# Third layer of a four-layer network: where the two tail steps of a region stand in the stream of matrix products

## The chip, the cores and the metric

One core of a Trainium2 chip runs the whole program. The metric is device time in microseconds (us), the median of several executions. TensorE (PE) does the matrix products, VectorE (DVE) and ScalarE (ACT) the elementwise work, GpSimd (POOL) a few copies, and SyncE (SP) issues the transfers.

## What is computed

Four layers over 1040 tokens (16 meta tokens and 1024 of the input) of width 1024: sliding-window attention, a matrix LSTM, a gated linear recurrence (HGRN2), and attention again. The change lies in the third. Per head, with chunks of tokens, its recurrence is, cut to what matters:

```python
def step(S, inp):
    q_, k_, v_, lf = inp
    A = jnp.cumsum(lf, axis=2)
    o_inter = jnp.einsum('bhtd,bhde->bhte', q_ * jnp.exp(A), S)
    dec = jnp.where(causal[..., None], A[:, :, :, None, :] - A[:, :, None, :, :], -jnp.inf)
    att = jnp.einsum('bhtd,bhtsd,bhsd->bhts', q_, jnp.exp(dec), k_)
    o = o_inter + jnp.einsum('bhts,bhse->bhte', att, v_)
    A_last = A[:, :, -1]
    S_new = jnp.exp(A_last)[..., None] * S + jnp.einsum('bhsd,bhse->bhde', k_ * jnp.exp(A_last[:, :, None] - A), v_)
    return S_new, o
```

The output of a chunk needs the state S that the chunk before it left. Before the recurrence the inputs are projected, after it the output is normed, gated with silu(z) and projected back.

## The kernel before, in words

Tokens lie in the columns: a block of 16 (block 0) and eight blocks of 128, in three column chunks of 400, 384 and 256. Each projection multiplies three times (high and low halves of the operands, `proj` L237, `proj_v` L271, `proj_out` L308). These products fill TensorE, and the recurrence of the third layer is woven between them.

`layer_c` (L1049) treats eight heads (0 to 7 here). A head has five regions (`REGIONS`, L1126): block 0 alone, then four pairs of blocks. `mixer` (L1128) makes two lists of steps for each region r. The main list holds eight level steps (`level`, L1139: DVE and ACT make the scaled keys and queries X), one burst of small products (`levels_mm`, L1181) and `tail0` (L1185), which masks and sums the products into the matrix `att` (DVE L1195 and L1204, POOL copies L1206, ACT copies L1208 and L1210) and makes the scaled queries `qA` and keys `kA`. The tail list holds `tail1` (L1222: TensorE transposes `kA` into PSUM, L1228, and ACT copies that to `kT`, L1230), a lag of 500, and for each block of the region one `tail2` (L1232). A `tail2` issues three products: `att` with the values (L1243), the scaled queries with the state S (L1245), and keys with values (L1250). From the last one DVE makes the next state (L1253 and L1255). One `kT` tile and two S tiles exist; PSUM has eight tiles for all uses.

Each step is a list of a cost, a function and a load. `weave` (L53) merges two lists so that both advance in proportion to their summed costs. The tail list of region r is woven with the main list of region r+1, behind a lag of 2000 (`TAIL_LAG`); the result is woven with the projections of the next head (the fill). The order of TensorE's instructions is exactly this order. The other engines' orders come from the framework's scheduler, which takes steps marked by `hi` (L356) early. Every engine runs its own instructions in that order and waits where an operand is missing. `pause` (L768) is a function that does nothing; the second layer already uses it as a step that counts in a weave and is taken out behind it.

Of the kernel before, what the change touches and what calls it, by code (L numbers as in the profile page):

```python
# [15 lines left out]
P = 128  # L16
# [5 lines left out]
NB = 9  # L22
# [7 lines left out]
def blk(b):  # L30
    return (0, NMETA) if b == 0 else (NMETA + P * (b - 1), P)
# [5 lines left out]
TAIL_LAG = 2000.0  # L37
# [1 line left out]
ROWS, TMPS, RAWS, YS, QS = 9, 5, 2, 3, 6  # L39
XS = 14  # L40
GAP, BURST, PAUSE = 200.0, 1300.0, 2500.0
KT_LAG = 500.0
NORM_AT = (4000.0, 0.7), (5000.0, 0.5), (8000.0, 0.5)
Y_LAST, Y_EARLY, Y_AHEAD = 3, 8, 2500.0
PARTS = 2, 2, 2
# [7 lines left out]
def weave(a, b):  # L53

    ta, tb = sum(x[0] for x in a) + 1e-9, sum(x[0] for x in b) + 1e-9
    out, i, j, ca, cb = [], 0, 0, 0.0, 0.0
    while i < len(a) or j < len(b):
        if j >= len(b) or (i < len(a) and ca / ta <= cb / tb):
            ca += a[i][0]
            out.append(a[i])  # L60
            i += 1
        else:
            cb += b[j][0]
            out.append(b[j])
            j += 1
    return out


def flat(groups):
    return [x for grp in groups for x in grp]  # L70


def outs(groups):

    first, out = groups[0]
    out = list(out)
    for splits, grp in groups[1:]:
        out.insert(len(out) - Y_EARLY, splits[0])
        out.insert(len(out) - Y_LAST, splits[1])
        out += grp  # L80
    return first, out
# [27 lines left out]
def hybrid_kernel(ctx: ExitStack, tc: tile.TileContext, ins, out, layers=(0, 1, 2, 3)):  # L109
    nc = tc.nc  # L110
    v, s, g, pe, sp = nc.vector, nc.scalar, nc.gpsimd, nc.tensor, nc.sync
# [11 lines left out]
    def nm(x):  # L123
        ctr[0] += 1
        return f"{x}{ctr[0]}"

    def row():
        return rpool.tile([P, T], F32, tag="r", name=nm("r"), bufs=ROWS)
# [13 lines left out]
    def psum(tag, bufs):  # L142
        return ps.tile([P, 512], F32, tag="p", name=nm(tag), bufs=8)
# [4 lines left out]
    def psa():  # L148
        return psum("pa", 1)
# [206 lines left out]
    def hi(fn):  # L356
        def f():
            with tc.high_priority(offset=PRIO):
                fn()

        return f
# [687 lines left out]
    def layer_c(i, j, fin):  # L1049
# [78 lines left out]
        def mixer(h):  # L1128
            vs = slice((h % 2) * P, (h % 2) * P + P)
            W = {}  # L1130
# [101 lines left out]
            def tail2(r, b):  # L1232
                blkno = REGIONS[r][b]
                c0, cn = blk(blkno)
                n = [blkno in z for z in CHUNK_BLOCKS].index(True)
                if blkno == CHUNK_BLOCKS[n][0]:
                    if n == 0:
                        R["o", h] = row()
                    W["po"] = psum("po", 1)
                oc = slice(c0 - CHUNKS[n][0], c0 - CHUNKS[n][0] + cn)  # L1240
                V = R["v", h // 2, blkno]
                att = W["att", r] if r == 0 else W["att", r][:, b, :]
                pe.matmul(W["po"][:, oc], V[:cn, vs], att, start=True, stop=(r == 0))  # L1243
                if r:
                    pe.matmul(W["po"][:, oc], W["S"], W["qA", r][:, P * b : P * b + P], start=False, stop=True)  # L1245
                if blkno == CHUNK_BLOCKS[n][-1]:
                    o_evac(n)
                if blkno < NB - 1:
                    pc = psa()
                    pe.matmul(pc[:, :P], W["kT", r][:cn, P * b : P * b + P], V[:cn, vs], start=True, stop=True)  # L1250
                    Sn = R["mix"].tile([P, P], F32, tag="S", name=nm("S"), bufs=2)
                    if r == 0:
                        v.tensor_copy(Sn, pc[:, :P])  # L1253
                    else:
                        v.scalar_tensor_tensor(Sn, W["S"], W["eL", r][:, b : b + 1], pc[:, :P],  # L1255
                                               op0=ALU.mult, op1=ALU.add)
                    W["S"] = Sn

            def o_evac(n):
                c0, cn = CHUNKS[n]  # L1260
                s.copy(R["o", h][:, c0 : c0 + cn], W["po"][:, :cn])
                W["sq", n] = sq = tmp()
                s.activation(sq[:, :cn], W["po"][:, :cn], AF.Square)
# [9 lines left out]
            def S(cost, fn, *a):  # L1273
                return [cost, hi(lambda: fn(*a)), None]

            main, tails = [], []
            for r in range(5):
                lvs = list(range(8)) if r else [3, 4, 5, 6, 7]
                st = []
                for lv in lvs:  # L1280
                    st.append(S(0.0, level, r, lv))
                    st.append([GAP, lambda: None, None])
                st.append(S(BURST if r else 0.2 * BURST, levels_mm, r, lvs))
                st.append(S(0.0, tail0, r))
                main.append(st)
                ts = [S(214 if r else 107, tail1, r), [KT_LAG, lambda: None, None]]
                for b in range(len(REGIONS[r])):
                    ts.append(S(640, tail2, r, b))
                    if REGIONS[r][b] in (5, 8):
                        ts.append(S(666, o_stat, 0 if REGIONS[r][b] == 5 else 1))  # L1290
                tails.append(ts)
# [10 lines left out]
        body = qg[0][0] + qg[0][1]  # L1302
        last = []
        for h in range(8):
            fill = qg[0][2] if h == 0 else []
            if h in (4, 6):
                fill += flat(outs(oc[h - 3]))
            if h < 7:
                fill += flat(fg[h + 1]) + flat(qg[h + 1])
            if h in (1, 3, 5):  # L1310
                fill += flat(vg[h // 2 + 1])
            for z in {2: (0, 1), 4: (2,), 5: (3,), 7: (4, 5, 6)}.get(h, ()):
                fill += flat(zg[z])
            main, tails, end = mixer(h)
            if h:
                tails[0].append(held)
            held = end
            mx = []
            for r in range(5):
                mx += weave(main[r], last)  # L1320
                last = [[TAIL_LAG, lambda: None, None]] + tails[r]
            body += weave(mx, fill)
        body += weave(last + [held], flat(zg[7]))
        return head, body, oc[5], oc[7]

    steps = []
# [4 lines left out]
    for pos, i in enumerate(layers):  # L1331
# [10 lines left out]
        if i % 3 == 0:  # L1342
            head, body, oa, ob = layer_a(i, i // 3, tail is None, i == 3, fin)
        elif i % 3 == 1:
            head, body, oa, ob = layer_b(i, i // 3, fin)
        else:
            head, body, oa, ob = layer_c(i, i // 3, fin)
# [158 lines left out]
```

## Time and profile before

| | us |
|---|---|
| median of 3 runs | 2607.71 (2605.75 to 2611.24) |
| the profiled execution | 2610.83 |
| its span, first to last instruction | 2609.0 |
| PE busy in the span | 2558.0 (98%) |
| DVE busy | 1980.3 (76%) |
| ACT busy | 1725.9 (66%) |
| POOL busy | 154.1 (6%) |

The span is the time from the first to the last instruction of the profiled execution; 1.8 us of that execution lie outside it. PE is the matrix products, PEld the loading of their stationary operand, which runs beside them. The third layer's recurrence takes the stretch from about 1611 to 2120 us of the span, some 62 us per head.

### The profile page before, as it was taken

What the parts mean: (1) busy time and instruction counts of PE and PEld (TensorE: products, weight loads), DVE (VectorE), ACT (ScalarE), POOL (GpSimd) and SP (SyncE); (2) the same over time, 40 slices, a digit from 0 to 9 for tenths busy, and PEclk for the clock granted to TensorE, in tenths of its full rate; (3) what the DMA queues carried; (4) which work ended last, traced back from release to release, by engine and by line L of the source; (5) the groups of instructions that cost most, each with busy time, mean ns of one, the idle gap of its engine ahead of it and who ended that gap; (6) DMA issues with size and microseconds to landing.
All of it is one profiled execution on the core that took longest, in us unless ns stands there. A gap on an engine that the chain in (4) does not pass through costs nothing.

```text
span 2609.0 us, 56062 instructions
## 1 busy us (share of the span) xinstructions
PE 2558.0 (98%) x21048; PEld 2459.0 (94%) x21048; DVE 1980.3 (76%) x5487; ACT 1725.9 (66%) x4757; POOL 154.1 (6%) x538
## 2 busy tenths in 40 slices
PE   7999999999999999999999999999999999999999
PEld 6899889899999999999999999999999999999999
DVE  6677777986767676767677788978787978677776
ACT  6777776566464646464646857878585867768872
POOL 1100100000000000000000000201001011000000
PEclk9999999999999999999999999999999999999999
DMA  4111111021111111111110101011110111111112
GB/s 136 56 43 50 46 37 47 17 67 58 41 58 41 58 41 58 41 58 41 55 61 34 57 27 42 30 38 34 34 42 26 42 62 45 54 44 47 53 38 82
DMA packets 74048, 126.81 MB, mean 49 GB/s; under 512 B 11552, under 2 KB 25760, under 8 KB 73776
## 3 DMA queue, kind: packets, MB, share of 16 engines
q1 hardware_dynamic: 73776, 123.23, 14.5%
q8 instruction: 165, 2.70, 0.4%
q14 instruction: 107, 0.88, 0.1%
HBM read 108.34 MB, written 4.26 MB: 43 GB/s over the span
## 4 chain that ended last, share of the span: by engine, by line
PE 81%; DVE 10%; ACT 6%; issue 1%; DMA 1%; POOL 0%; SPq 0%; DVEq 0%; ACTq 0%; POOLq 0%
PE pj L254 39%; PE pj L337 16%; PE pj L299 11%; PE po L682 2%; PE pt L660 1%; PE pm L614 1%; PE pm L615 1%; DVE t L407 1%; PE pa L534 1%; DVE ul L188 1%; PE po L918 1%; PE pj L295 1%; PE pm L890 1%; DVE X L1153 1%; DVE X L1155 1%
## 5 line engine op out<-in xcount | busy, mean ns | idle before, releaser
L254 PE MATMUL pj<-uh,wh 128*128 128x384 f32 (+2 forms) x2592 | 870.9, 336 | 3.7 <-ACT uh L187 3.6
L254 PE MATMUL pj<-ul,wh 128*128 128x384 f32 (+2 forms) x2592 | 835.3, 322 | 2.9 <-DVE ul L188 2.8
L254 PE MATMUL pj<-uh,wl 128*128 128x384 f32 (+2 forms) x2592 | 832.9, 321 | 0.1
L254 PEld LDWEIGHTS pj<-uh,wh 128*128 128x128 f32 x2592 | 491.3, 190 | 24.1 <-issue 12.7
L254 PEld LDWEIGHTS pj<-ul,wh 128*128 128x128 f32 x2592 | 491.2, 190 | 8.7 <-DVE ul L188 5.5
L254 PEld LDWEIGHTS pj<-uh,wl 128*128 128x128 f32 x2592 | 490.9, 189 | 0.5 <-DVE wl L188 0.4
L188 DVE TENSOR_TENSOR wl<-wr,wh 128x512 fp32r<-128x512 f32 x336 | 227.9, 687 | 58.1 <-ACT wh L187 55.4
L340 DVE TENSOR_TENSOR x<-x,pj 128x384 f32<-128x384 f32 (+2 forms) x480 | 235.4, 510 | 43.2 <-PE pj L337 41.3
L187 ACT CAST wh<-wr 128x512 fp32r<-128x512 f32 x337 | 203.3, 616 | 83.0 <-PE pj L337 26.8
L299 PE MATMUL pj<-wh,uh 128*128 128x256 f32 x896 | 258.1, 288 | 0.0
L337 PE MATMUL pj<-yh,wh 128*128 128x384 f32 (+2 forms) x768 | 253.0, 329 | 0.0
L299 PE MATMUL pj<-wh,ul 128*128 128x256 f32 x896 | 252.4, 282 | 0.0
L299 PE MATMUL pj<-wl,uh 128*128 128x256 f32 x896 | 252.3, 282 | 0.0
L337 PE MATMUL pj<-yl,wh 128*128 128x384 f32 (+2 forms) x768 | 247.4, 322 | 3.1 <-DVE yl L188 3.1
L337 PE MATMUL pj<-yh,wl 128*128 128x384 f32 (+2 forms) x768 | 246.8, 321 | 0.0
L299 PEld LDWEIGHTS pj<-wh,uh 128*128 128x128 f32 x896 | 169.3, 189 | 1.1 <-issue 0.3
L187 ACT CAST yh<-r 128x400 fp32r<-128x400 f32 (+2 forms) x144 | 68.6, 477 | 153.2 <-PE pj L337 141.7
L299 PEld LDWEIGHTS pj<-wl,uh 128*128 128x128 f32 x896 | 169.3, 189 | 0.5
L299 PEld LDWEIGHTS pj<-wh,ul 128*128 128x128 f32 x896 | 169.3, 189 | 0.0
L428 ACT ACTIVATE t<-t 128x384 f32<-128x384 f32 (+2 forms) x240 | 117.8, 491 | 76.5 <-DVE t L427 74.8
L427 DVE SCALAR_TENSOR_TENSOR t<-pj,t 128x384 f32<-128x384 f32 (+2 forms) x192 | 98.8, 514 | 78.2 <-ACT t L426 75.3
L337 PEld LDWEIGHTS pj<-yl,wh 128*128 128x128 f32 x768 | 144.9, 189 | 5.0 <-DVE yl L188 4.7
(265 smaller groups left out, 5431.4 us busy)
## 6 DMA issues: line engine op xcount, KB each, us to landing
wr<-in_b_win SPq DMA_DIRECT2D x128, 256.0 KB, 2.6
wr<-in_a_win SPq DMA_DIRECT2D x80, 256.0 KB, 2.7
wr<-in_c_win SPq DMA_DIRECT2D x64, 256.0 KB, 2.7
r<-rowsd SPq DMA_DIRECT2D x16, 520.0 KB, 5.4
wr<-in_a_wout SPq DMA_DIRECT2D x32, 256.0 KB, 2.7
wr<-in_b_wout SPq DMA_DIRECT2D x32, 256.0 KB, 2.6
t<-t SPq DMA_DIRECT2D x96, 48.0 KB, 1.9
wr<-in_c_wout SPq DMA_DIRECT2D x16, 256.0 KB, 2.7
```

The lines of the kernel that those rows point to most:

```text
L187: s.copy(h, src)
L188: v.tensor_tensor(l, src, h.bitcast(F32), op=ALU.subtract)
L254: pe.matmul(acc[:, :cn], a[:, k, :], b[:, k, c0 : c0 + cn], start=(k == 0 and i == 0), stop=(k == KT - 1 and i == 2))
L295: pe.matmul(acc[:48, :256], um[:, k, :], m[:, kk, :], start=(k == 0 and m is wh), stop=(k == KT - 1 and m is wl))
L299: pe.matmul(acc[:cn, :256], a[:, k, c0 : c0 + cn], m[:, kk, :], start=(k == 0 and i == 0), stop=(k == KT - 1 and i == 2))
L337: pe.matmul(acc[:, :cn], a[:, k, mc], b, start=(k == 0 and i == 0), stop=(k == 1 and i == 2))
L340: v.tensor_tensor(x[:, m, c0 : c0 + cn], x[:, m, c0 : c0 + cn], acc[:, :cn], op=ALU.add)
L407: v.scalar_tensor_tensor(u, x[:, k, cs], ngain[:, self.i, k : k + 1], self.acc[n], op0=ALU.mult, op1=ALU.mult)
L427: v.scalar_tensor_tensor(a[:, :cn], z, 0.0, a[:, :cn], op0=ALU.min, op1=ALU.subtract)
L428: s.activation(a[:, :cn], a[:, :cn], AF.Exp)
L534: pe.matmul(st[:, 2 * k : 2 * k + 2], sq[:, z : z + P], R["masks"][:, 0:P:64], start=True, stop=True)
L682: pe.matmul(po[64 * hh : 64 * hh + 64, q0 - c0 : q0 - c0 + nq], V[kb][:kn, vc : vc + 64], ws[hh]["Pt"][:kn, u, ki, :nq], start=(ki == 0), ...
```

## The change

Two constants are new. A pause of 1500 stands between the two `tail2` steps of a region, and a pause of 600 is added to the lag ahead of a tail list. Both count when the lists are woven and are taken out of the body afterwards. Inside a `tail2` the product of keys and values (now L1246) is issued ahead of the product with the state (now L1248); the new state is made on DVE as before (now L1254 and L1256).

```diff
-KT_LAG = 500.0
+KT_LAG, S_LAG, TAIL_MORE = 500.0, 1500.0, 600.0
...
                 pe.matmul(W["po"][:, oc], V[:cn, vs], att, start=True, stop=(r == 0))
+                if blkno < NB - 1:
+                    pc = psa()
+                    pe.matmul(pc[:, :P], W["kT", r][:cn, P * b : P * b + P], V[:cn, vs], start=True, stop=True)
                 if r:
                     pe.matmul(W["po"][:, oc], W["S"], W["qA", r][:, P * b : P * b + P], start=False, stop=True)
                 if blkno == CHUNK_BLOCKS[n][-1]:
                     o_evac(n)
                 if blkno < NB - 1:
-                    pc = psa()
-                    pe.matmul(pc[:, :P], W["kT", r][:cn, P * b : P * b + P], V[:cn, vs], start=True, stop=True)
...
                 for b in range(len(REGIONS[r])):
+                    if b:
+                        ts.append([S_LAG, pause, None])
                     ts.append(S(640, tail2, r, b))
...
-                last = [[TAIL_LAG, lambda: None, None]] + tails[r]
+                last = [[TAIL_LAG, lambda: None, None], [TAIL_MORE, pause, None]] + tails[r]
...
         body += weave(last + [held], flat(zg[7]))
+        body = [z for z in body if z[1] is not pause]
```

Three places of the built order follow; L254 and L299 are projection products. First TensorE in head 1, region 2, before: the two blocks' tail steps (`att`, S, keys with values).

```order
L1228 MATMUL pt4019_22250<-ident_75,X4005_22152 128x128 x2
L1168 MATMUL pm4021_22255<-X4007_22158 32x64 x4
...
L1243 MATMUL po3966_21878<-att3725_20158,v3753_20361 128x128
L1245 MATMUL po3966_21878<-X4004_22149,S4001_22135 128x128
L1250 MATMUL pa4026_22345<-v3753_20361,kT4020_22251 128x128
L1243 MATMUL po4028_22349<-att3725_20158,v3762_20445 128x128
L1245 MATMUL po4028_22349<-X4004_22149,S4027_22347 128x128
L1250 MATMUL pa4029_22352<-v3762_20445,kT4020_22251 128x128
```

The same place now:

```order
L1228 MATMUL pt4017_22233<-ident_75,X4005_22152 128x128 x2
...
L1243 MATMUL po3961_21861<-att3725_20158,v3753_20361 128x128
L1246 MATMUL pa4021_22256<-v3753_20361,kT4018_22234 128x128
L1248 MATMUL po3961_21861<-X4004_22149,S4000_22121 128x128
L1168 MATMUL pm4024_22264<-X4007_22158 32x64 x4
...
L1243 MATMUL po4028_22349<-att3725_20158,v3762_20445 128x128
L1246 MATMUL pa4029_22351<-v3762_20445,kT4018_22234 128x128
L1248 MATMUL po4028_22349<-X4004_22149,S4023_22262 128x128
```

The first block's step has moved ahead of the next region's burst (L1168), with 12 projection products between the transposes and it where a burst and 24 products stood; between the two steps the burst and 24 projection products now stand.

Second, TensorE in head 1, region 4, before, from the transposes (L1228) to the first `tail2`:

```order
L1228 MATMUL pt4079_22696<-ident_75,X4069_22631 128x128 x2
L254 MATMUL pj4085_22711<-uh_84,wh4040_22422 128x384
...
L1243 MATMUL po4087_22723<-att3725_20158,v3775_20576 128x128
L1245 MATMUL po4087_22723<-X4068_22628,S4065_22614 128x128
L1250 MATMUL pa4088_22726<-v3775_20576,kT4080_22697 128x128
```

The same place now:

```order
L1228 MATMUL pt4079_22696<-ident_75,X4069_22631 128x128 x2
L1243 MATMUL po4086_22716<-att3725_20158,v3775_20576 128x128
L1246 MATMUL pa4087_22718<-v3775_20576,kT4080_22697 128x128
L1248 MATMUL po4086_22716<-X4068_22628,S4065_22614 128x128
L254 MATMUL pj4089_22723<-uh_84,wh4040_22422 128x384
```

Six projection products of 384 columns that stood between the transposes and the step are gone from there.

Third, DVE in head 1, region 4, before, around the mask (L1195) and the sum (L1204) that POOL copies into `att`:

```order
L1152 TENSOR_TENSOR X4109_22863<-r3916_21568,r3917_21569 128x64x2
L1153 TENSOR_TENSOR X4109_22863<-r3916_21568 128x64x2
L1195 TENSOR_TENSOR t4066_22616<-pm4056_22506,masks3718_20129 128x192 x2
L1255 SCALAR_TENSOR_TENSOR S4065_22614<-S4060_22586,s4036_22385,pa4064_22612 128x128
L1204 TENSOR_REDUCE rd4067_22619<-t4066_22616 128x64
```

The same place now:

```order
L1256 SCALAR_TENSOR_TENSOR S4065_22614<-S4056_22501,s4036_22385,pa4063_22608 128x128
L1152 TENSOR_TENSOR X4109_22863<-r3916_21568,r3917_21569 128x64x2
L1153 TENSOR_TENSOR X4109_22863<-r3916_21568 128x64x2
L1195 TENSOR_TENSOR t4066_22616<-pm4058_22512,masks3718_20129 128x192 x2
L1155 TENSOR_TENSOR X4109_22863<-X4109_22863,Q3956_21848 128x64x2
L1204 TENSOR_REDUCE rd4067_22619<-t4066_22616 128x64
```

The state has moved ahead of the mask, and one step of the levels stands between mask and sum.

## Rows read from the trace of the kernel before

**Rows 1.** The page: busy time of the engines, share of the span.

```profile
PE 2558.0 (98%) x21048; PEld 2459.0 (94%) x21048; DVE 1980.3 (76%) x5487; ACT 1725.9 (66%) x4757; POOL 154.1 (6%) x538
```

**Rows 2.** Busy time by stretch: start:end, length, engines, PEclk, DMA share, GB/s.

```profile
1620.00:1640.00 20.00, 16.91 (x313) 16.00 (x314) 18.73 (x63) 17.68 (x52) 2.21 (x8) 1.00 0.01 2
1640.00:1650.00 10.00, 9.78 (x101) 9.38 (x101) 8.83 (x34) 7.16 (x22) 2.98 (x4) 0.83 0.01 2
2020.00:2060.00 40.00, 38.73 (x565) 37.49 (x564) 37.22 (x130) 33.06 (x96) 2.82 (x8) 1.00 0.12 41
2060.00:2100.00 40.00, 37.99 (x556) 35.72 (x555) 36.40 (x122) 34.04 (x95) 5.05 (x12) 1.00 0.09 29
```

**Rows 3.** Waits, PEld, 1615 to 1640, head 0: us in total, times, longest.

```profile
PEld pm L1178 <- DVE X L1155: 2.6, 1, 2.6
PEld pa L1250 <- ACT kT L1230: 1.4, 1, 1.4
PEld po L1245 <- DVE S L1255: 0.8, 1, 0.8
```

**Rows 4.** Waits, PEld, then PE, 1640 to 2002, rest of head 0 to head 5.

```profile
PEld po L1245 <- DVE S L1255: 4.0, 9, 0.5
...
PE po L1245 <- DVE S L1255: 2.3, 9, 0.3
```

**Rows 5.** Waits, PEld, then PE, 2002 to 2125, heads 6 and 7.

```profile
PEld po L1245 <- DVE S L1255: 3.1, 2, 1.6
...
PEld po L1243 <- POOL att L1206: 0.9, 1, 0.9
...
PE po L1245 <- DVE S L1255: 2.7, 2, 1.4
```

**Rows 6.** Timeline, PE, head 1, region 2: start us, us, instruction [idle before].

```profile
1702.07 0.28 PE L299 MATMUL pj<-wh,uh 128*128 128x256 f32 x1
1702.19 0.28 PE L299 MATMUL pj<-wl,uh 128*128 128x256 f32 x1
...
1702.43 0.38 PE L1243 MATMUL po<-att,v 128*128 128x128 f32 x2
1702.65 0.39 PE L1245 MATMUL po<-X,S 128*128 128x128 f32 x2
...
1703.10 0.39 PE L1243 MATMUL po<-att,v 128*128 128x128 f32 x2
1703.70 0.49 PE L1245 MATMUL po<-X,S 128*128 128x128 f32 x2 [0.22 <-DVE S L1255]
```

**Rows 7.** Timeline, PE, then ACT, head 2, region 4: transposes, kT, its user.

```profile
1785.83 0.38 PE L1228 MATMUL pt<-ident,X 128*128 128x128 f32 x2
...
1787.55 0.39 PE L1250 MATMUL pa<-v,kT 128*128 128x128 f32 x2
...
1786.43 0.37 ACT L1230 COPY kT<-pt 128x256 f32<-128x256 f32 x1
```

**Rows 8.** Timeline, PE, then ACT, head 2, region 0.

```profile
1735.52 0.27 PE L1228 MATMUL pt<-ident,X 128*16 128x128 f32 x1
...
1736.15 0.24 ACT L1230 COPY kT<-pt 16x128 f32<-16x128 f32 x1
```

**Rows 9.** Timeline, PE, then ACT, head 6, region 4.

```profile
2060.18 0.38 PE L1228 MATMUL pt<-ident,X 128*128 128x128 f32 x2
...
2062.03 0.35 ACT L1230 COPY kT<-pt 128x256 f32<-128x256 f32 x1
```

**Rows 10.** Timeline, POOL, then PE, head 1, region 4.

```profile
1721.88 2.23 POOL L1206 COPY att<-rd 32x64 f32<-32x64 f32 x4 [15.04 <-DVE rd L1204]
...
1725.09 0.38 PE L1243 MATMUL po<-att,v 128*128 128x128 f32 x2
```

**Rows 11.** Timeline, POOL, then DVE, head 1, region 2.

```profile
1689.44 5.75 POOL L1206 COPY att<-rd 32x64 f32<-32x64 f32 x4 [8.50 <-DVE rd L1204]
...
1691.42 1.08 DVE L1155 TENSOR_TENSOR X<-X,Q 128x128 f32<-128x128 f32 x5
```

## The prediction

> **What bounds the kernel now.** I read the page's busy shares first: TensorE is busy for 98% of the span and no other engine for more than 76% [rows 1]. So a wait of PE is time, and a wait elsewhere is time only if PE comes to wait for it. Next the waits of PE and of its weight load, PEld, in the stretch that the change touches, in three pieces because DVE's load differs between them. At the start of head 0 there are three, 4.8 us in all: for X 2.6, for `kT` 1.4, for the state S 0.8 [rows 3]. From 1640 to 2002 only S is worth the name, 4.0 us in nine waits [rows 4]. In heads 6 and 7 it is S again, 3.1 us in two, and `att` from POOL, 0.9 us once [rows 5]. The whole prize is therefore some 9 us of 2600, and the question is what the moved instructions wait for in its place. Last the busy time by stretch: DVE is busy for 18.7 us of 20 from 1620 to 1640, and for 37.2 and 36.4 us of 40 from 2020 to 2100 [rows 2]. There a wait for S is partly a wait for DVE as such, and removing one brings another.
>
> The sum is made against the profiled execution, 2610.8 us (span 2609.0), which stands 3.1 above the median of the three runs, 2607.7. The difference that comes out is taken from the median.
>
> **What is removed and added.** Nothing is computed more or less: TensorE issues the same products, DVE, ACT and POOL the same operations, SP the same transfers. The pauses issue nothing. All costs are in waits.
>
> **The state's waits, 1640 to 2002.** Before, the second block's step followed the first directly: keys with values, then `att` with values, then the S product, at 0.22 us per tail product where nothing waits (1702.43 to 1702.65) [rows 6]. The state was asked for some 0.4 us after the product that makes it. In the stalled step `att` to S took 0.60 us (1703.10 to 1703.70), 0.38 more [rows 6], so the state is there some 0.8 us after that product. Now a burst and 24 projection products of 256 columns stand between; one of those takes 0.12 us (1702.07 to 1702.19) [rows 6], so the distance is 2.9 us and the burst. The smallest distance in any region, worked the same way, is about that too. DVE would have to be 2 us late to bring the wait back. So these nine go. Their worth: PEld's rows say 4.0 us, PE's own rows 2.3 [rows 4]; the start-to-start loss of 0.38 in the stalled step, where PE shows 0.22 idle [rows 6], is nearer to PEld's 4.0 / 9 = 0.44. I take PEld's, and 0.07 more for each wait, since the product behind a wait takes 0.49 and not 0.39 us [rows 6] and not all of that is overlapped: **-4.6 us** (ends -2.3 and -4.6).
>
> [...]
>
> **The state's waits, heads 6 and 7.** 3.1 us in two [rows 5], 3.2 with the extra, in a stretch where DVE is busy 91 to 93% [rows 2]. All of it comes back if DVE catches up during the 2.9 us, none if DVE has a backlog that only shows somewhere else. I take half: **-1.6 us** (0 to -3.2).
>
> **Head 0's start.** The three waits [rows 3] follow from DVE at 94% [rows 2]. The tail steps come earlier relative to the burst, DVE's work does not shrink; a wait that shrinks at S reappears at the next burst's X. [...] I take **+0.4 us**.
>
> **New: the wait for `kT`.** Ahead of the keys-with-values product the S product and, before region 4, six products no longer stand. In head 1, region 4, the distance from the first transpose is two transposes and `att`: 3 x 0.22 = 0.66 us. ACT's copy is ready 0.97 us after the first transpose where nothing is in its way (1785.83 to 1786.80) [rows 7]; region 0 has one transpose, a distance of 0.44 and a copy ready after 0.87 (1735.52 to 1736.39) [rows 8]. Three region 0s (heads 1, 3, 7) stand at 0.44: 3 x (0.43 + 0.07) = 1.5. Heads 1 (region 4) and 5 (region 1) stand at 0.66: 2 x (0.31 + 0.07) = 0.8. Head 6, region 4, too, but there the step waits longer for `att`; head 0, region 1, is in the term above. Seven others at 0.97 to 1.54 us get 0.3 together. Of forty copies four need more than 1.7 us, the longest 2.20 (2060.18 to 2062.38) [rows 9]; for such in places now at 1.7 to 2.1 us I add 0.6. Together **+3.2 us**. Ends: if each of the five had the shortest, 0.8, it would be 1.4; if each had the longest, 8.7. I stay near the typical row, for ACT is 66% busy [rows 1].
>
> **New: the wait for `att`.** In head 1, region 4, POOL is done at 1724.11 and `att` is used at 1725.09 [rows 10], 0.98 us to spare. The six products of 384 columns that went away stood ahead of it, and at 0.18 us each the use comes 1.06 us sooner: to spare, nothing. Head 6, region 4, waits 0.9 already [rows 5] and asks 1.1 sooner. DVE makes the sum that POOL copies no earlier, and one step of the levels now stands between mask and sum. **+1.0 us**, 0.9 of it in head 6 (0 to 3.3, the upper end if `att` also comes 1 us later in the four tightest regions).
>
> **Sum.** -4.6 - 1.6 + 0.4 + 3.2 + 1.0 = -1.6 us: 2610.8 becomes 2609.2, the median 2607.7 becomes **2606.1**. Queues: no DMA is issued by a moved step, SP and POOL keep their order beyond the copies named. Work that is queued behind a waiting tail step is the fill of projections, which nobody awaits soon; PE just loses the time.
>
> **Rivals.**
> 1. *The stalls go and nearly nothing comes in their place.* DVE in heads 6 and 7 is not full, and the copies to `kT` take their shortest: -4.6 - 3.2 - 0.9 (S in head 0) + 1.4 = -7.3, 2600.4. For it: DVE has 2.8 us of slack in 40 at the worst place [rows 2] and the wait there is 1.6 at most at a time [rows 5]. Against it: distances of 0.44 us cannot cover 0.87 [rows 8].
> 2. *Slower: POOL's copies of `att` fall beside DVE's two-operand run.* Four copies take 2.23 us in one region [rows 10] and 5.75 in another, where DVE runs the levels' products L1155 beside them [rows 11]: 3.5 us longer. The change puts just such a step next to the sum that feeds the copies. Region 4 of heads 1 and 6 has no margin left, so each such slowing is 3.5 us of PE. It decides from two on: -1.6 + 7.0 = +5.4, 2613.1; with head 7's region 4, 2616.6. Against it: in before most of the copies escape, DVE's order near them moves by one or two steps, and a step may move off them too.
>  [...]
> 3. *The wait only moves, from S to `kT`.* This is a part of the forecast; at its upper end, 8.7 in place of 3.2, the sum is +3.9, 2611.6.
> 4. *The change doesn't do what it says.* The built order shows the steps apart and the products exchanged. Chance nil.
>
> **Numbers.** A measurement here tells 0.2%, 5.2 us: faster is below 2602.5, slower above 2612.9. The forecast with rival 3 gets 0.60, rival 1 gets 0.27, rival 2 0.13. The forecast's own ends lie within the bound: upward 2611.6 as in rival 3, downward 2606.1 - 1.6 - 1.8 - 1.0 (all of heads 6 and 7, shortest `kT`, no `att` wait) = 2601.7, of which a little is past it; that part is in rival 1's chance. The range reaches from rival 1's time, with a little of the clock term, 2600.0, to 2612.0, and leaves out rival 2 and a sliver below.
>
> **What would show it.** Right: no wait of PEld for S from 1640 on; for `kT` 3 us in seven to ten waits, region 0 of heads 1, 3 and 7 first; for `att` 1 to 2 us in region 4; head 0's start still near 4.8 us. Wrong: any S wait of 0.3 us that stays between two tail steps; `kT` waits above 6 us or below 1; POOL copies above 5 us in region 4 (rival 2); heads 6 and 7 shorter by more than 3 us (rival 1).

## The result, and the profile after

The changed kernel takes 2613.57 us (median of 22 runs, 2609.09 to 2621.18), the kernel before 2609.24 in as many (2605.12 to 2612.41). The ratio is 1.0016, 95% interval 1.0010 to 1.0022: slower by 4.3 us, which is 0.16%. The forecast was 2606.1 with a range up to 2612.0, so the time lies above the range and the small movement went the other way. (The three runs of the kernel before that the forecast started from had a median 1.5 us below that of the 22.)

The page of the changed kernel, busy time of the engines, answers to [rows 1]. Nothing is computed more, and the 2.6 us that the span grew (2609.0 to 2611.6) are not in it:

```profile
span 2611.6 us, 56035 instructions
...
PE 2557.9 (98%) x21048; PEld 2458.1 (94%) x21048; DVE 1980.0 (76%) x5487; ACT 1724.0 (66%) x4757; POOL 154.0 (6%) x538
```

The waits of PEld in the changed kernel (us in total, times, longest), first 1615 to 1640, then 1640 to 2002, then 2002 to 2125. They answer to [rows 3], [rows 4] and [rows 5]:

```profile
PEld po L1243 <- POOL att L1206: 1.8, 2, 1.2
PEld pa L1246 <- ACT kT L1230: 0.6, 1, 0.6
PEld pm L1178 <- ACT X L1146: 0.5, 1, 0.5
...
PEld pa L1246 <- ACT kT L1230: 7.3, 6, 2.2
...
PEld po L1243 <- POOL att L1206: 0.9, 2, 0.8
...
PEld po L1243 <- POOL att L1206: 2.9, 3, 2.2
PEld pa L1246 <- ACT kT L1230: 2.5, 5, 0.8
```

No wait for S is left, in any piece, heads 6 and 7 included; 7.9 us of them stood there before. Head 0's start has lost its long wait for X too. But `kT` is now waited for 10.4 us in 12 places, where it was 1.4 in one, and `att` 5.7 us in seven, where it was 0.9 in one. (Over the whole stretch, 1611 to 2125, the view gives 10.4 and 5.7.) The waits removed were the ones forecast; those that came are larger than what they replaced.

The step of [rows 6], head 1, region 2, in the changed kernel (PE timeline: start us, us, instruction): six products at 0.22 us from start to start, and no idle time:

```profile
1695.32 0.38 PE L1243 MATMUL po<-att,v 128*128 128x128 f32 x2
1695.54 0.39 PE L1246 MATMUL pa<-v,kT 128*128 128x128 f32 x2
1695.76 0.39 PE L1248 MATMUL po<-X,S 128*128 128x128 f32 x2
...
1700.39 0.38 PE L1243 MATMUL po<-att,v 128*128 128x128 f32 x2
1700.61 0.39 PE L1246 MATMUL pa<-v,kT 128*128 128x128 f32 x2
1700.83 0.39 PE L1248 MATMUL po<-X,S 128*128 128x128 f32 x2
```

Now the longest of the new waits, head 3, region 0, PE:

```profile
1798.52 0.27 PE L1228 MATMUL pt<-ident,X 128*16 128x128 f32 x1
1798.72 0.39 PE L1243 MATMUL po<-att,v 16*128 16x16 f32 x2
1801.22 0.48 PE L1246 MATMUL pa<-v,kT 16*128 16x128 f32 x2 [2.11 <-ACT kT L1230]
```

and what ACT does meanwhile:

```profile
1798.23 0.51 ACT L1100 ACTIVATE t<-t,one 128x256 f32<-128x256 f32 x1
1798.64 0.74 ACT L1220 ACTIVATE s<-r 128x1 f32<-128x1 f32 x7
1799.65 0.42 ACT L1154 ACTIVATE X<-X 128x256 f32<-128x256 f32 x1 [0.27 <-DVE X L1153]
1799.99 0.52 ACT L1220 ACTIVATE s<-r 128x1 f32<-128x1 f32 x2
1800.53 0.50 ACT L424 ACTIVATE t<-pj 128x400 f32<-128x400 f32 x1
1800.93 0.24 ACT L1230 COPY kT<-pt 16x128 f32<-16x128 f32 x1
```

The copy itself takes 0.24 us, as in [rows 8]. It stands in ACT's order behind small exponentials for the tails (L1220), one of a level (L1154) that itself waited 0.27 us for DVE, and the first operation of a sigmoid (L424). The transpose was done near 1798.8, the copy was started at 1800.93. Before the change the same region's copy was done 0.93 us after its transpose began (1797.54 to 1798.47), behind one running operation; now it took 2.65. PE, then ACT, before:

```profile
1797.54 0.27 PE L1228 MATMUL pt<-ident,X 128*16 128x128 f32 x1
...
1797.73 0.60 ACT L1100 ACTIVATE t<-t,one 128x384 f32<-128x384 f32 x1
1798.23 0.24 ACT L1230 COPY kT<-pt 16x128 f32<-16x128 f32 x1
```

The wait has an aftermath. The busy time by stretch of the changed kernel (start:end, length, PE, PEld, DVE, ACT, POOL, PEclk, ...) shows the granted clock below full in the two stretches of 5 us at and behind that wait, and full in all four of [rows 2], of which one is shown:

```profile
1640.00:1650.00 10.00, 9.28 (x162) 8.49 (x161) 9.60 (x41) 7.97 (x29) 1.25 (x4) 1.00 0.07 24
1800.00:1805.00 5.00, 3.78 (x15) 3.48 (x16) 4.54 (x15) 3.55 (x12) 1.12 (x4) 0.79 0.00 0
1805.00:1810.00 5.00, 5.00 (x32) 5.00 (x32) 3.74 (x12) 2.71 (x8) 0.00 (x0) 0.87 0.35 106
```

By the granted clock 5 x 0.21 + 5 x 0.13 = 1.7 us are lost, just what the kernel before lost behind its wait for X near 1640 [rows 2]. The clock's loss moved and did not change in size.

### The profile page after: what moved, and what is told of

Same layout as the page of the kernel before. It is cut to its first block, busy times and chain, and to the rows that moved or that the text cites. A ratio compares the mean times of both kernels' runs of the same rounds, so it can differ in the third digit from the quotient of the medians.

```text
span 2611.6 us, 56035 instructions
## 1 busy us (share of the span) xinstructions
PE 2557.9 (98%) x21048; PEld 2458.1 (94%) x21048; DVE 1980.0 (76%) x5487; ACT 1724.0 (66%) x4757; POOL 154.0 (6%) x538
## 4 chain that ended last, share of the span: by engine, by line
PE 79%; DVE 10%; ACT 7%; issue 1%; DMA 1%; POOL 1%; SPq 0%; DVEq 0%; ACTq 0%; POOLq 0%
PE pj L254 37%; PE pj L337 16%; PE pj L299 11%; PE po L682 2%; PE pt L660 1%; PE pm L614 1%; DVE t L407 1%; PE pm L615 1%; PE pa L534 1%; PE pj L295 1%; DVE ul L188 1%; PE po L918 1%; ACT Sm L639 1%; PE pm L1178 1%; ACT wh L187 1%
## 5 line engine op out<-in xcount | busy, mean ns | idle before, releaser
L254 PE MATMUL pj<-uh,wh 128*128 128x384 f32 (+2 forms) x2592 | 872.3, 337 | 3.9 <-ACT uh L187 3.9
L254 PE MATMUL pj<-ul,wh 128*128 128x384 f32 (+2 forms) x2592 | 836.1, 323 | 2.9 <-DVE ul L188 2.7
L254 PE MATMUL pj<-uh,wl 128*128 128x384 f32 (+2 forms) x2592 | 833.1, 321 | 0.1
L254 PEld LDWEIGHTS pj<-uh,wh 128*128 128x128 f32 x2592 | 491.5, 190 | 24.9 <-issue 13.1
L254 PEld LDWEIGHTS pj<-ul,wh 128*128 128x128 f32 x2592 | 491.5, 190 | 8.7 <-DVE ul L188 5.4
L254 PEld LDWEIGHTS pj<-uh,wl 128*128 128x128 f32 x2592 | 491.3, 190 | 0.5 <-DVE wl L188 0.4
L299 PE MATMUL pj<-wh,uh 128*128 128x256 f32 x896 | 257.6, 288 | 0.0
L299 PE MATMUL pj<-wh,ul 128*128 128x256 f32 x896 | 251.9, 281 | 0.0
L299 PE MATMUL pj<-wl,uh 128*128 128x256 f32 x896 | 251.9, 281 | 0.0
L299 PEld LDWEIGHTS pj<-wh,uh 128*128 128x128 f32 x896 | 168.6, 188 | 1.1 <-issue 0.3
L299 PEld LDWEIGHTS pj<-wl,uh 128*128 128x128 f32 x896 | 168.7, 188 | 0.5
L299 PEld LDWEIGHTS pj<-wh,ul 128*128 128x128 f32 x896 | 168.8, 188 | 0.0
```

What stands on the lines that cost most here:

```text
L254: pe.matmul(acc[:, :cn], a[:, k, :], b[:, k, c0 : c0 + cn], start=(k == 0 and i == 0), stop=(k == KT - 1 and i == 2))
L299: pe.matmul(acc[:cn, :256], a[:, k, c0 : c0 + cn], m[:, kk, :], start=(k == 0 and i == 0), stop=(k == KT - 1 and i == 2))
```

## The experiments

The theory after the result: what the state gave back was taken by `kT`, because the transposes now stand too close to the product that reads it, and by `att`. Its rivals: the exchange of the two products costs by itself; the other place of the tail steps among the projections costs; the clock does. Every time is a median, and every ratio is against the kernel before in runs on the same chip. Waits are PEld's from 1611 to 2125. "Asked" is the time from the first transpose of a region to the start of the product reading `kT`, less that product's wait; "ready" is from the first transpose to the end of the copy. Both are worked out from the timelines of the forty regions.

**The exchange alone** (only_product_ahead): the kernel before with the product of keys and values ahead of the state's, without pauses. The edit is shown against the changed kernel.

```diff
-KT_LAG, S_LAG, TAIL_MORE = 500.0, 1500.0, 600.0
+KT_LAG = 500.0
...
-                    if b:
-                        ts.append([S_LAG, pause, None])
...
-                last = [[TAIL_LAG, lambda: None, None], [TAIL_MORE, pause, None]] + tails[r]
+                last = [[TAIL_LAG, lambda: None, None]] + tails[r]
...
-        body = [z for z in body if z[1] is not pause]
```

> No pauses; in each tail step the product of keys and values stands ahead of the product with the state, as in the change. Theory (the change loses by waits for the copy to kT, which the pauses cause by bringing the tail step up to its transposes): the transposes stay 1.7 us or more ahead, the distance to kT shrinks by 0.22 us only, the state is asked for 0.22 us or more later, so of the 7.9 us of waits for S in 12 places some 2 to 3 us go; kT stays below 2 us; 2607 (0 to 3 us below the kernel before). Rival (putting the product ahead is itself what costs, since it asks for kT first): waits for kT of 5 us or more, and 2 us or more above the kernel before.

Measured: 2608.09, 2.1 below the kernel before; ratio 0.9991 (0.9982 to 0.9999). Waits for S 4.5 us in 8, for `kT` 2.1 in 2, for `att` 1.8 in 2. `kT` is a little above the 2 us of the theory. The exchange is not what costs: alone it takes no time and may gain a little, for its interval ends just below 1.

**The pauses alone** (only_pauses): the changed kernel with the two products in their old order.

```diff
-                if blkno < NB - 1:
-                    pc = psa()
-                    pe.matmul(pc[:, :P], W["kT", r][:cn, P * b : P * b + P], V[:cn, vs], start=True, stop=True)
                 if r:
                     pe.matmul(W["po"][:, oc], W["S"], W["qA", r][:, P * b : P * b + P], start=False, stop=True)
...
                 if blkno < NB - 1:
+                    pc = psa()
+                    pe.matmul(pc[:, :P], W["kT", r][:cn, P * b : P * b + P], V[:cn, vs], start=True, stop=True)
                     Sn = R["mix"].tile([P, P], F32, tag="S", name=nm("S"), bufs=2)
```

> Both pauses, but in each tail step the product with the state stands ahead of the product of keys and values, as before. Theory: the waits for kT in 12 places shrink by 0.22 us each, from 10.4 to about 8 us, those for att stay near 5.6, no wait for S; 2 us below the changed kernel, 1 to 3 above the kernel before. Rival (the product ahead is what costs): kT waits below 2 us, 2604 or less.

Measured: 2610.98; ratio 1.0006 (0.9997 to 1.0014), 0.8 us above the kernel before. `kT` 7.3 us in 9, `att` 5.5 in 4, S none. The waits are as the theory had them. That the time lies above the kernel before is not shown, since the interval holds 1; what is shown is that the new waits come with the pauses.

**A longer lag behind the transposes** (longer_kt_lag).

```diff
-KT_LAG, S_LAG, TAIL_MORE = 500.0, 1500.0, 600.0
+KT_LAG, S_LAG, TAIL_MORE = 1500.0, 1500.0, 600.0
```

> The changed kernel with the lag between the transposes and the first tail step raised from 500 to 1500. By the built order the distance from the first transpose to the product that reads kT is 2.3 us or more everywhere but in head 6, region 4 (1.8), the state stays 1.6 us or more behind the product that makes it, and att is used 0 to 5 us later than in the changed kernel. Theory (kT and att waits took what the state gave back): waits for S under 0.5 us, for kT under 2, for att 1 to 3; 2602 to 2604, 5 to 7 below the kernel before. Rival (what costs is the other place of the tail steps among the projections, or the clock, not these waits): within 2 us of the changed kernel, 2612 or more, with the waits gone.

Measured: 2601.89; ratio 0.9968 (0.9956 to 0.9979), 8.3 us below the kernel before. Its waits:

```profile
PEld po L1243 <- POOL att L1206: 3.3, 2, 2.7
...
PEld pm L1178 <- DVE X L1155: 1.9, 1, 1.9
PEld po L1248 <- DVE S L1256: 1.7, 3, 1.0
```

No wait of note for `kT` is left; S is back with 1.7, which the theory had not expected. One constant turns a kernel that is slower than before into the one with the lowest time here. But it makes `att` asked for later as well, so it doesn't yet tell the two waits apart. The next two runs do.

**A longer lag ahead of the tail lists** (longer_tail_lag): `att` is used about as late as before the change, and `kT` is asked for within 0.8 us of the transposes in 13 regions (4 in the changed kernel).

```diff
-KT_LAG, S_LAG, TAIL_MORE = 500.0, 1500.0, 600.0
+KT_LAG, S_LAG, TAIL_MORE = 500.0, 1500.0, 2600.0
```

> The changed kernel with the pause ahead of a tail list raised from 600 to 2600. att is now used as late as before the change or later, but the transposes come late too, so 16 places have only 0.44 to 0.66 us from the transposes to the product that reads kT (7 in the changed kernel). Theory (kT is the larger part of the loss): att waits under 1.5 us, kT waits 8 to 14 us in 15 or more places, none for S; 2609 to 2615. Rival (att is the larger part of the loss and the short distances to kT cost no more than the 0.4 us each that the prediction took): kT waits under 7 us, 2606 or less.

Measured: 2619.98; ratio 1.0037 (1.0025 to 1.0049), 9.8 us above the kernel before, worse than the theory's own range.

```profile
PEld pa L1246 <- ACT kT L1230: 17.0, 22, 1.6
...
PEld po L1243 <- POOL att L1206: 1.2, 1, 1.2
```

**The transposes earlier, the rest where it was** (early_transposes): what is taken from the lag ahead is given to the lag behind.

```diff
-KT_LAG, S_LAG, TAIL_MORE = 500.0, 1500.0, 600.0
+KT_LAG, S_LAG, TAIL_MORE = 1500.0, 1500.0, -400.0
```

> The changed kernel with 1000 taken from the lag ahead of the transposes (pause of 600 becomes -400) and given to the lag behind them (500 becomes 1500): the sums are the same, so the tail steps stand where the changed kernel has them, within a product or two (att 0 to 0.9 us earlier), and only the transposes stand some 2 us further ahead. Theory (waits for kT alone are the larger part of the loss, independent of att): kT waits fall from 10.4 to below 3 us, att waits stay at 5 to 8 us; 2604 to 2607. Rival (the gain of the longer lag came from the later att, or from less crowding of the tail step): 2610 or more although the kT waits are gone.

Measured: 2604.02; ratio 0.9980 (0.9970 to 0.9990), 6.5 us below the kernel before.

```profile
PEld po L1243 <- POOL att L1206: 7.4, 7, 2.5
...
PEld pa L1246 <- ACT kT L1230: 1.7, 3, 1.0
PEld pm L1178 <- DVE X L1155: 1.7, 1, 1.7
```

This is the run that decides. The tail steps stand where the changed kernel has them, `att` is waited for even longer, and 8.7 us of waits for `kT` go. The region that waited 2.2 us shows how: asked 4.15 us after its transpose and ready after 1.05 (ACT timeline of this kernel; the transpose began at 1794.12). Here the copy is quick again as well; over all regions it is not, as a table below shows.

```profile
1794.02 0.60 ACT L1100 ACTIVATE t<-t,one 128x384 f32<-128x384 f32 x1
1794.53 0.50 ACT L1095 ACTIVATE t<-t,one 128x256 f32<-128x256 f32 x1
1794.93 0.24 ACT L1230 COPY kT<-pt 16x128 f32<-16x128 f32 x1
```

**Without the pause ahead of the tail lists** (no_tail_more), and **the pause between the steps alone** (only_s_lag, the same edit together with that of only_pauses, so that the products stand in their old order):

```diff
-KT_LAG, S_LAG, TAIL_MORE = 500.0, 1500.0, 600.0
+KT_LAG, S_LAG, TAIL_MORE = 500.0, 1500.0, 0.0
```

> The changed kernel without the pause ahead of the tail lists (600 to 0). att is used about 1 us earlier than in the changed kernel (2 us earlier than before the change in region 4 of heads 6 and 7, 3.4 in head 1), and region 0 of heads 1 to 7 has 3 us and more from its transposes to the product that reads kT, not 0.44 to 1.5. Theory: kT waits fall to 5 us or so (region 0 drops out), att waits rise to 9 us or more; 2612 to 2616, within 3 us of the changed kernel. Rival (att has slack, its waits are accidents of DVE's order): att waits stay below 6 us, 2609 or less.

> The pause between the two tail steps alone: no pause ahead of the tail lists, and the product with the state ahead of that of keys and values, as before. Theory: no wait for S; kT waits about 0.6 us fewer than the 1.9 of the version with the product ahead (0.22 us further from the transposes), att waits near its 9.5; 2604 to 2606. Rival (the product ahead is needed for the gain): S waits of 2 us or more stay, 2607 or more.

Measured: 2605.00 (ratio 0.9978, 0.9969 to 0.9987) and 2604.12 (0.9980, 0.9971 to 0.9989). The first misses the theory's time by 7 us and its `kT` by 3: 1.9 us are left, not 5. The `att` waits came as expected, yet the kernel is fast. The waits of only_s_lag:

```profile
PEld po L1243 <- POOL att L1206: 9.1, 10, 1.8
...
PEld pa L1250 <- ACT kT L1230: 2.0, 3, 1.1
```

So the parts of the change can be set side by side:

| pause between steps | pause ahead | product ahead | ratio to before | 95% interval | S | kT | att |
|---|---|---|---|---|---|---|---|
| 0 | 0 | no | 1 | | 7.9 | 1.4 | 0.9 |
| 0 | 0 | yes | 0.9991 | 0.9982 to 0.9999 | 4.5 | 2.1 | 1.8 |
| 1500 | 0 | no | 0.9980 | 0.9971 to 0.9989 | 0 | 2.0 | 9.1 |
| 1500 | 0 | yes | 0.9978 | 0.9969 to 0.9987 | 0 | 1.9 | 9.5 |
| 1500 | 600 | no | 1.0006 | 0.9997 to 1.0014 | 0 | 7.3 | 5.5 |
| 1500 | 600 | yes | 1.0016 | 1.0010 to 1.0022 | 0 | 10.4 | 5.7 |

The pause between the steps does what it was read to do, 0.2% faster. The pause of 600 ahead of the lists costs 0.26 to 0.38%, some 7 to 10 us, more than it is easy to see in it: it trades about 4 us of waits for `att` for 5 to 8.5 of waits for `kT`. In region 0 of heads 1 to 7 it moves "asked" from 3.4 to 5.1 us (no_tail_more) down to 0.6 to 1.5 (changed). The pause ahead was not run without the pause between the steps, so its cost is shown only beside that one.

The clock, the third rival, carries little of these differences. The span times the part of the clock that was not granted, averaged over all runs of a kernel, is 9.7 to 10.5 us for the kernel before in three sets of runs, 10.9 for the changed kernel, 8.7 for early_transposes and 9.4 for longer_kt_lag. That is at most 1.2 us of the changed kernel's 4.3, 1.6 of the 6.5 and 1.1 of the 8.3.

**Only region 0 mended** (region0_lag).

```diff
-                ts = [S(214 if r else 107, tail1, r), [KT_LAG, lambda: None, None]]
+                ts = [S(214 if r else 107, tail1, r), [KT_LAG if r else 1500.0, lambda: None, None]]
```

> The changed kernel with the lag of 1500 behind the transposes in region 0 alone, 500 elsewhere: region 0 has 3.8 us or more from its transposes to the product that reads kT, where the changed kernel has 0.44 to 1.54; its three waits of region 0 in heads 1, 3 and 7 were 1.5, 2.2 and 0.8 or less of its 10.4 us of kT waits, and the clock fell behind the 2.2. Theory (places add up): kT waits 5 to 7 us, att waits 5 to 7; 2607 to 2611. Rival (kT's waits move on to the next regions, since ACT stays as far behind): kT waits 8 us or more, 2612 or more.

Measured: 2614.45; ratio 1.0019 (1.0009 to 1.0028). A miss of both: `kT` falls to 3.7 us, more than expected, but `att` rises to 10.7 in nine, one of 3.5, and the time stays. Behind two of the waits the clock fell, near 1628 and 2037:

```profile
1625.00:1630.00 5.00, 1.83 (x13) 1.61 (x16) 3.30 (x10) 1.77 (x4) 1.22 (x4) 0.78 0.09 30
...
2035.00:2040.00 5.00, 3.14 (x17) 2.68 (x17) 4.31 (x11) 3.25 (x11) 1.33 (x4) 0.74 0.00 0
```

The longer lag in region 0 makes the list of that region longer, and so moves the regions beside it: in heads 1 to 7, region 1 uses `att` up to some 2 us sooner after its burst than in the changed kernel. But the new waits do not stand there. The 3.5 us stand in head 0, region 1, where the sum on DVE ended 9.3 us after its burst (3.2 in the changed kernel), and 2.1 in head 6, region 2 (9.9 against 2.8). Why DVE made these sums later isn't shown. A lag here isn't a local repair.

**The copy on DVE** (kt_by_dve), the same order on TensorE:

```diff
-                s.copy(kT[:bn, :w], pt[:bn, :w])
+                v.tensor_copy(kT[:bn, :w], pt[:bn, :w])
```

> The changed kernel with the copy to kT on DVE in place of ACT; TensorE's order is the same. Theory (the copy is late because it stands in ACT's queue behind what ACT has not done yet; five to eight operations at the three longest waits): the three waits of 1.5 to 2.2 us (head 1 and head 3, region 0; head 4, region 2) shrink to below 1 us each or go, and others come where DVE is behind; in all 6 to 14 us of kT waits. Rival (the way from PSUM through any engine takes as long, its queue matters little): the same places with the same waits within 0.3 us.

Measured: 2615.95; ratio 1.0022 (1.0013 to 1.0031), `kT` 12.0 us in 17, `att` 7.3 in 8. The three places named now wait 1.5, 1.2 and 1.1 us where they waited 1.5, 2.2 and 1.9. Two are shorter, none is under 1: neither theory nor rival. Over all places the waits are no smaller on DVE's queue (12.0 us against 10.4), so moving the copy to another engine is no remedy here. How much of the delay is the queue and how much the rest of the way is not separated by this run.

**Mask and sum earlier on DVE** (sum_first), the changed kernel with these in a block of higher priority:

```diff
+SUM_PRIO = 120
...
                 for b in range(nb):
-                    v.tensor_tensor(t6[:bn, b, f0:, :w], pf[:bn, b, f0:, :w], mk[:bn, f0:, :w], op=ALU.mult)
+                    with tc.high_priority(offset=SUM_PRIO):
+                        v.tensor_tensor(t6[:bn, b, f0:, :w], pf[:bn, b, f0:, :w], mk[:bn, f0:, :w], op=ALU.mult)
...
-                    v.tensor_reduce(rd, t6.rearrange("p b l t -> p b t l"), axis=mybir.AxisListType.X, op=ALU.add)
-                    for g0 in range(0, P, 32):
-                        g.tensor_copy(att[g0 : g0 + 32, :, g0 : g0 + 32], rd[g0 : g0 + 32])
+                    with tc.high_priority(offset=SUM_PRIO):
+                        v.tensor_reduce(rd, t6.rearrange("p b l t -> p b t l"), axis=mybir.AxisListType.X, op=ALU.add)
+                        for g0 in range(0, P, 32):
+                            g.tensor_copy(att[g0 : g0 + 32, :, g0 : g0 + 32], rd[g0 : g0 + 32])
```

> The changed kernel with mask, sum and POOL's copies of att given a higher place in the scheduler's order: TensorE's and POOL's orders are the same, DVE takes mask and sum earlier. Theory (att is late because DVE makes the sum late): att waits fall from 5.7 to 3 us or less, kT waits stay at 9 to 12; 2610 to 2612. Rival (POOL's copies themselves are what is late): att waits stay at 5 us or more, 2613 or more.

Measured: 2612.42; ratio 1.0013 (1.0004 to 1.0022), `att` 5.7 us in 8, `kT` 11.8 in 12. By its number this is the rival, but the run doesn't decide: at the longest wait, head 6, region 4, the mask stands behind the same operations on DVE as without the edit (two of the levels, the state's and two that read a projection), so there the edit did nothing.

**Towards a faster version** (both_lags, with the lags 1500, 1500 and 1600; kt_lag_sum_first, longer_kt_lag with the edit of sum_first):

```diff
-KT_LAG, S_LAG, TAIL_MORE = 500.0, 1500.0, 600.0
+KT_LAG, S_LAG, TAIL_MORE = 1500.0, 1500.0, 1600.0
```

> The version with the lag of 1500 behind the transposes, and the pause ahead of the tail lists raised from 600 to 1600 too. att is used later than there in region 1 and in region 4 of heads 2 and 7, at the same distance in head 6, region 4; transposes to kT has six places of 1.5 to 2.0 us, where the version with the one lag has one. Theory: att waits 1 to 3 us, kT waits 1 to 3, S below 2; 2601 to 2604, within 2 us of the version with the one lag. Rival (a later att is worth more than the distance to kT): 2599 or less.

> The version with the lag of 1500 behind the transposes, with mask and sum earlier on DVE as well. Theory: of its 3.3 us of att waits (2.7 in head 6, region 4) 1 to 2 are left, the wait for X at the start stays, kT below 1; 2599 to 2601, the fastest. Rival (DVE, busy for 93% there, pays elsewhere: X or S): 2602 or more with the same sum of waits.

Measured: 2604.99 (0.9980, 0.9971 to 0.9989) and 2602.82 (0.9973, 0.9962 to 0.9984). Neither has a lower ratio than longer_kt_lag, though the intervals overlap. In all three the wait for `att` in head 6, region 4, stays at 2.7 us; so moving the mask in DVE's order, as far as this priority did, gained nothing.

## Why the prediction was wrong

**The state's waits: right.** -4.6 and -1.6 were taken, the lower end of the second was -3.2. All 12 waits went. That half of heads 6 and 7 would come back somewhere else was right in kind: those two heads now wait 2.5 us for `kT` and 2.9 for `att`, where 4.0 us stood for S and `att` [rows 5].

**Head 0's start: of the other sign.** The term was +0.4 us, and it said that a wait which shrinks at S reappears at X. No run of the changed kernel shows this term: the waits from 1615 to 1640 fell from 4.8 us [rows 3] to 2.9, that is -1.9. Of the clock term, which the lower end of the range counts in part, nothing came here either: the clock stayed full (1.00 from 1620 to 1650), and the 1.7 us that the kernel before lost near 1640 [rows 2] were lost again, but in head 3.

**The wait for `kT`: the step that failed.** The prediction put it: "I stay near the typical row, for ACT is 66% busy". It forecast 3.2 us beside head 0; from 1640 on 9.8 were measured, above the 6 us that the prediction itself named as a sign of being wrong. The five places that it priced one by one, at 2.3 us, waited 4.8: heads 1 and 3, region 0, 1.5 and 2.2. All others, priced at 0.9, waited 5.0: head 4, region 2, alone 1.9. The distances come from the built order and were near (0.59 us measured in the three region 0s, 0.44 forecast). The time until the copy is ready was not. It was taken from the kernel before, 0.87 and 0.97 us, and a mean busy share was used as the reason why it would stay. Over the forty regions:

| | asked, mean | ready, mean | ready after 1.7 us or more |
|---|---|---|---|
| before | 4.5 | 1.06 | 4 |
| changed | 1.6 | 1.36 | 12 |
| no_tail_more | 2.3 | 1.24 | 6 |
| early_transposes | 3.2 | 1.43 | 13 |
| longer_kt_lag | 4.7 | 1.50 | 13 |

Add up, region by region, what "ready" exceeds "asked". Old copies with old distances give 1.3 us, old copies with the new distances 1.4, the new copies with the old distances 1.6, new with new 7.9. Neither of the two makes the loss, only both together. The prediction set the new distances against the old copies, and that is why it looked cheap. With early transposes or the longer lag the copies are as late as in the changed kernel or later, 13 of 40 at 1.7 us or more, and hardly any is waited for (1.7 us in three places, and none of note), since they are asked for 3 to 5 us after.

Why the copies are later is visible in ACT's rows, in part. At the three longest waits (head 1 and head 3, region 0; head 4, region 2) ACT starts six, nine and eight operations between the end of the transposes and the copy; before the change it started none in the first two of these regions and two in the third. In the rows of head 3, region 0, the transpose is done 2.1 us before the copy starts, and ACT does other work first (L1220, L1154, L424). Where the copy stands in ACT's order is the scheduler's choice; why it put it further back here was not tried.

**The wait for `att`: the mechanism right, the size wrong.** The term was 1.0 us, 0.9 of it in head 6; 4.8 came (5.7 against 0.9). Head 6, region 4, waits 2.2 us, 1.3 more, near what the term said; but regions 1 and 2 of head 0 wait 1.8 us together, and head 6, region 3, 0.5, which the text had not looked at, and head 1, region 4, whose margin came out as nothing, waits 0.8. PE's own rows see 4.0 of the 5.7.

**Rival 2** has its 2613.1 near the measured time by chance, for its mechanism isn't what happened. POOL's four copies take 1.2 to 2.3 us in 28 of 32 regions, 3.2 in one where 0.6 us is waited, 4.4 in one and 5.4 in two; `att` in these last three was not waited for. At the longest `att` wait they took 2.0 us, and DVE's sum ended 8.7 us after the burst (9.1 in the kernel before). **Rival 3**, the wait that moves to `kT`, is what came: it was held to be at most 8.7 us in place of 3.2, and was counted with the forecast.

**The sum, with what was measured**: S -7.9, X -2.3 (2.8 to 0.5), `kT` +9.0, `att` +4.8, clock 0: +3.6. The profiled executions differ by 2.6 (2613.47 and 2610.83), the medians by 4.3.

**What stays open.** Sums of waits follow the times of the kernels only roughly, to 2 to 4 us: only_s_lag has 2 us less of waits than the kernel before and is 5.8 us faster, longer_tail_lag some 7 more and is 9.8 slower, and sum_first has more of them than region0_lag and the lower ratio. Waits for `att` seem to cost less than their rows, those for `kT` more; a profile is one execution and can't settle it. Head 6, region 4, waits for `att` in every kernel. In the changed one `att` isn't late there: it is ready 10.9 us after the end of its burst, and in region 4 of heads 1 to 5 after 10.7 to 11.1. It is asked for soonest, 8.7 us after the burst, where the other heads ask after 9.7 to 12.8. In longer_kt_lag it is asked for after 10.4 and ready only after 13.0, and why it is late in that kernel was not found.

## What to carry to other kernels

A step that is brought closer to the operand it needs must be priced with how late that operand can be when the producing engine is in the middle of something else, not with how fast it was when there was time to spare: with slack, the trace of the kernel before showed the typical delay, and its long ones cost little (1.7 us or more in 4 of 40 regions, with 1.4 us of waits for `kT` in all); without it 12 of 40 were that long, and the waits came to 10.4 us. Where two lists are woven by share, a pause moves the steps of the list and of the lists beside it; look at each distance that matters (here transposes to copy, sum to `att`, product to state) after every edit. If a change has several parts, run them apart: here one part gained 0.2% and another lost more.

## What was not expected of the hardware

In these runs TensorE's clock did not fall behind every long wait. Behind the waits of 2.6 us (before) and 2.2 us (changed) the granted clock was 0.50 for 3.4 us (1640.0 to 1643.4 and 1802.9 to 1806.3), which is 1.7 us lost each time; behind the wait of 2.5 us for `att` in early_transposes, near 2057, the row shows it full (1.00) up to 2060. The wait for `att` in head 6, region 4, of 2.7 us in longer_kt_lag and in both_lags, has a fall at it in the first (0.85 and 0.81) and none up to 2060 in the second (1.00). The row of early_transposes, two of longer_kt_lag, one of both_lags:

```profile
2055.00:2060.00 5.00, 2.94 (x18) 2.76 (x18) 3.05 (x9) 2.49 (x7) 1.10 (x4) 1.00 0.16 54
...
2050.00:2055.00 5.00, 2.60 (x13) 2.26 (x12) 3.87 (x12) 3.62 (x9) 1.10 (x4) 0.85 0.33 105
2055.00:2060.00 5.00, 5.00 (x33) 4.26 (x33) 3.55 (x12) 2.77 (x9) 0.00 (x0) 0.81 0.01 3
...
2055.00:2060.00 5.00, 4.01 (x33) 3.72 (x34) 2.85 (x9) 3.76 (x9) 0.81 (x3) 1.00 0.16 50
```

So these two kernels, with the same wait, differ there by 1.7 us of clock (5 x 0.15 + 5 x 0.19), a third of the 0.2% that the prediction took as what a measurement tells. The fastest kernel lost 1.7 us in this way too, so its gain isn't the clock's.
